# A macaron transformer layer: the first block product of each FFN gets its raw weights and weight sums in a small pool of its own, and its split operands in other buffers

## The chip, the cores and the metric

The kernel runs on one core of a Trainium2 chip. The metric is the device time of one execution in microseconds (us), as the median of several runs. The engines are named as in the profile: PE (matmuls), DVE (VectorE), ACT (ScalarE), POOL (GpSimd) and SP (which here only issues DMAs).

## The reference

One layer: a SwiGLU FFN, a mixer (stick-breaking attention and RWKV-7 side by side), and a second SwiGLU FFN, each between RMSNorms and added to the residual. The change touches the two FFNs alone:

```python
def swiglu(x, w_gate, w_up, w_down):
    return (jax.nn.silu(x @ w_gate) * (x @ w_up)) @ w_down

f = swiglu(rmsnorm(x, ffn1_pre_g[l]), ffn1_w_gate[l], ffn1_w_up[l], ffn1_w_down[l])
x = x + 0.5 * rmsnorm(f, ffn1_post_g[l])
m = hybrid_mixer(...)
x = x + rmsnorm(m, mix_post_g[l])
f = swiglu(rmsnorm(x, ffn2_pre_g[l]), ffn2_w_gate[l], ffn2_w_up[l], ffn2_w_down[l])
x = x + 0.5 * rmsnorm(f, ffn2_post_g[l])
```

Here x is 1024 tokens by 1024 channels in float32, and the hidden width is 2816.

## The kernel before

**Precision.** Every float32 matmul is made of three: each operand is split into a high part (`wh`, `xh`) and the rest (`wl`, `xl`), and `mm3` (lines 118 to 121) adds high x high, high x low and low x high. So each weight tile takes a rounding copy and a subtraction, nearly all of them on POOL (the copy on ACT for three of seven operands).

**The up phase.** The hidden width is 22 blocks of 128 (`f` = 0 to 21). Blocks 0 and 1 are *plain*: `plain_mm(f, h)` multiplies the whole gate and up weights of a block with half h of the tokens, and `plain_evac` takes SiLU(gate) x up to DRAM. Two of these four calls come before `up()`, two in it. Blocks 2 to 21 are *block products*: for each block, the gate and up weights and the two token halves form a 2 x 2 block matrix product, done with 7 half-size products (Winograd's form) in place of 8. One half-size product is 12 matmuls of 512 columns, a block takes 84. This needs sums on both sides:

- the **input sums**, once for each FFN: `combine()` (lines 231 to 267) makes them from the normalised input on DVE, with whole tiles of 128 x 2048 in a pool of five (`xr`), their high parts on ACT. It is a generator: `up()` runs it in three pieces between the plain products;
- the **weight sums**, once for each block: `prep(f)` (lines 291 to 309) makes S1 to S4 on DVE (128 x 512 each) from the raw weights that `load(f)` fetched (two DMAs of 512 KB on SP's queue), and then splits the seven operands in the order `PO` = 1, 2, 5, 6, 4, 7, 3: the high part on ACT for 2, 6 and 7, else on POOL (line 307), and the low part always on POOL (line 308).

`product(f)` (lines 368 to 393) runs the seven products and the evacuations between them; `evac1` takes the first two (`p1`), `u2`, `y5`, `u3` are later ones.

**Buffers.** Split operands go in pairs into a ring of six tile pairs (`slot`, lines 280 to 286). Pool `WP` is always open and has two raw tiles (`wr`) and four `wh`/`wl` pairs; the plain blocks fill exactly these four. Pool `fu` of the up phase holds the rest: two pairs, the raw weights of even blocks (`raw`; odd blocks use `wr`), the weight sums (`S`) and the evacuation tiles (`tp`). `fu` is opened only when `combine()` is through, since its addresses overlap those of `xr`. The line that decides which pairs of the ring lie where is

```python
if j == 0:
    pool = self.fu if i % 6 < 2 else WP
```

**The down phase** follows at once: `ffn_down` loads the down weights through `wr` (two tiles) and splits them on POOL into `WP`'s four pairs, every third one into a pool of its own (`EX`).

**What sets the order.** A scheduler orders each engine's instructions when the program is built, following the order of the code, data and buffer dependencies; buffers of a pool are handed on in order of release. Each engine, and SP's queue, then executes in that fixed order and waits at its head.

Of the kernel before, what the change touches and what calls it, by code (L numbers as in the profile page):

```python
# [13 lines left out]
ALU = mybir.AluOpType  # L14
# [4 lines left out]
P = 128  # L19
# [11 lines left out]
def layer_kernel(ctx: ExitStack, tc: tile.TileContext, a: dict, out: bass.AP, dbg=None):  # L31
# [182 lines left out]
    class Ffn:  # L214
# [54 lines left out]

        def load(self, f):  # L270
            c = slice(f * P, (f + 1) * P)
            pool, tag = (WP, "wr") if f % 2 else (self.fu, "raw")
            pair = []
            for i, w in enumerate((self.wg, self.wu)):
                t = pool.tile(tag, f"{self.nm}r{i}_{f}", [P, 1024]).rearrange("p (k c) -> p k c", c=P)
                nc.sync.dma_start(t, w[:, :, c])
                pair.append(t)
            self.raw[f] = pair

        def slot(self):  # L280
            i, j = divmod(self.nslot, 2)
            self.nslot += 1
            if j == 0:
                pool = self.fu if i % 6 < 2 else WP
                self.pair = [pool.tile(t, f"{self.nm}{t}_{i}", [P, 1024], F32R) for t in ("wh", "wl")]
            return [self.half(t, j) for t in self.pair]

# [2 lines left out]

        def prep(self, f):
            G, U = self.raw.pop(f)
            S = [self.fu.tile("S", f"{self.nm}S{f}_{i}", [P, 1024]) for i in range(2)]
            S1, S2, S3, S4 = [self.half(S[i // 2], i % 2) for i in range(4)]
            A11, A12, A21, A22 = G[:, 0:4], G[:, 4:8], U[:, 0:4], U[:, 4:8]
            tt = nc.vector.tensor_tensor
            tt(S1, A21, A22, op=ALU.add)
            tt(S2, S1, A11, op=ALU.subtract)
            tt(S3, A11, A21, op=ALU.subtract)
            tt(S4, A12, S2, op=ALU.subtract)  # L300
            src = {1: A11, 2: A12, 5: S1, 6: S2, 4: A22, 7: S3, 3: S4}
            for n in PO:
                wh, wl = self.slot()
                if n in (2, 6, 7):
                    nc.scalar.copy(wh, src[n])  # L305
                else:
                    nc.gpsimd.tensor_scalar(wh, src[n], 1.0, 0.0, op0=ALU.mult, op1=ALU.add)  # L307
                nc.gpsimd.tensor_tensor(wl, src[n], wh, op=ALU.subtract)  # L308
                self.op[f, n] = wh, wl
# [84 lines left out]

        def up(self):

            comb = self.combine()
            self.plain_mm(0, 1)
            self.plain_evac(0, 0)
            self.plain_evac(1, 0)  # L400
            next(comb)
            self.plain_mm(1, 1)
            next(comb)
            self.plain_evac(0, 1)
            self.plain_evac(1, 1)
            next(comb, None)
            self.fu = Pool(self.nm + "u", dict(raw=2, S=2, wh=2, wl=2, tp=8))
            self.load(2)
            self.load(3)
            self.prep(2)  # L410
            for f in range(2, NF):
                if f + 1 < NF:
                    self.prep(f + 1)
                if f + 2 < NF:
                    self.load(f + 2)
                self.product(f)
            self.store(NF - 1)
            self.fu.close()

    def ffn_down(pl, hp, F, gb, post, half=None):  # L420
        nm = F.nm
# [170 lines left out]
    WP = Pool("wp", dict(wr=2, wh=4, wl=4))  # L592
# [11 lines left out]
    for h in range(2):  # L604
        for p2 in range(2):
# [3 lines left out]
            for i in range(2):  # L609
                tt = h * 4 + p2 * 2 + i  # L610
# [11 lines left out]
            r = rsqrt_col(nm, ss, 1.0 / D, EPS, n=2)  # L622
            for i in range(2):
                tt = h * 4 + p2 * 2 + i
# [419 lines left out]
    S2 = [pb.const(f"S{i}", [P, 4, P]) for i in range(2)]  # L1044
# [383 lines left out]
```

## Time and profile before

| | us |
|---|---|
| median of 3 runs (2266.04 to 2268.66) | 2267.11 |
| the profiled execution | 2267.87 |
| span of its instructions | 2266.1 |
| PE busy in it | 2142.8 (95%) |
| POOL busy | 963.7 (43%) |
| DVE busy | 1102.3 (49%) |

The profile is of one execution; its own time lies 0.76 us above the median of the runs and 1.8 us above its span. PE is busy for 95% of the span, so the time is PE's work plus its idle stretches, and each idle stretch is read where it lies: on the timeline, the bracket at a row's end gives how long the engine stood still before that instruction and what released it. Busy shares of the other engines say little; what counts is when a given operand of theirs is ready.

### The profile page before, as it was taken

Reading aid. Unit: us, or ns where it says so; the run is one execution under the profiler, and the core shown is the slowest. Engines: PE = TensorE matmul, PEld = TensorE weight load, DVE = VectorE, ACT = ScalarE, POOL = GpSimd, SP = SyncE. Lnnn points to the kernel's source line nnn. Section 1 sums busy time; section 2 is a strip of 40 time slices with the busy share of each in tenths; the row PEclk is TensorE's granted clock in tenths of the full one; section 3 lists DMA queues with packets and bytes.
Section 4 is the critical chain, followed back from the end, with each engine's and each line's share of the span. In section 5 each row is a group of like instructions: output and inputs, shape, how many; then the busy total and the mean of one; then the engine's idle time right before and its main releaser. Section 6 shows DMA issues by size and latency. Waiting matters only on the chain.

```text
span 2266.1 us, 29554 instructions
## 1 busy us (share of the span) xinstructions
PE 2142.8 (95%) x11168; PEld 1764.5 (78%) x11168; DVE 1102.3 (49%) x1652; ACT 786.0 (35%) x1349; POOL 963.7 (43%) x875
## 2 busy tenths in 40 slices
PE   7799999999999999999999999899799999999998
PEld 5678888878887777777888887777678888878886
DVE  4743333322445555735617778636743333322446
ACT  3322222223224544324126667436322222222212
POOL 2476666644232364344311111231666666634323
PEclk8899999999999999999989999999899999999999
DMA  3233232245444353353763663343232222245444
GB/s 116 70 93 91 75 90 75 67 142 183 142 149 130 93 164 119 109 168 99 229 161 117 187 200 108 130 139 121 76 91 84 84 84 84 66 137 169 130 135 162
DMA packets 295277, 276.16 MB, mean 122 GB/s; under 512 B 29664, under 2 KB 237536, under 8 KB 295136
## 3 DMA queue, kind: packets, MB, share of 16 engines
q1 hardware_dynamic: 244304, 248.85, 35.8%
q10 hardware_dynamic: 50832, 25.43, 4.2%
q8 instruction: 88, 1.44, 0.3%
q14 instruction: 53, 0.43, 0.1%
HBM read 195.60 MB, written 78.64 MB: 121 GB/s over the span
## 4 chain that ended last, share of the span: by engine, by line
PE 78%; DVE 10%; POOL 4%; ACT 4%; issue 3%; DMA 1%; SPq 0%; DVEq 0%; ACTq 0%; POOLq 0%
PE f1d L120 3%; PE f1d L121 3%; PE f1d L119 3%; PE pj L119 3%; PE f2d L119 3%; PE f2d L120 3%; PE f2d L121 3%; PE pj L121 3%; PE pj L120 3%; PE f2X L119 2%; PE f2X L120 2%; PE f2X L121 2%; PE f1X L119 2%; PE f1X L121 2%; PE f1X L120 2%
## 5 line engine op out<-in xcount | busy, mean ns | idle before, releaser
L107 POOL TENSOR_SCALAR wh<-wr 128x1024 fp32r<-128x1024 f32 x87 | 112.1, 1289 | 480.3 <-PE f1d L121 152.8
L108 POOL TENSOR_TENSOR wl<-wr,wh 128x1024 fp32r<-128x1024 f32 x87 | 213.5, 2455 | 6.0 <-PE pj L121 0.2
L120 PE MATMUL f1d<-wl,f1hh 128*128 128x512 f32 x352 | 138.8, 394 | 3.9 <-POOL wl L108 3.9
L119 PE MATMUL f2d<-wh,f2hh 128*128 128x512 f32 x352 | 137.9, 392 | 4.7 <-issue 3.5
L121 PE MATMUL f1d<-wh,f1hl 128*128 128x512 f32 x352 | 138.6, 394 | 0.4 <-DVE f1hl L435 0.4
L119 PE MATMUL f1d<-wh,f1hh 128*128 128x512 f32 x352 | 138.1, 393 | 0.0
L120 PE MATMUL f2d<-wl,f2hh 128*128 128x512 f32 x352 | 137.7, 391 | 0.0
L121 PE MATMUL f2d<-wh,f2hl 128*128 128x512 f32 x352 | 137.4, 390 | 0.0
L308 POOL TENSOR_TENSOR f2wl<-f2S,f2wh 128x512 fp32r<-128x512 f32 x80 | 104.0, 1311 | 4.0 <-ACT f2wh L305 1.7
L308 POOL TENSOR_TENSOR f1wl<-f1S,f1wh 128x512 fp32r<-128x512 f32 x80 | 103.9, 1310 | 4.0 <-ACT f1wh L305 1.7
L433 ACT CAST f2hh<-f2r 128x768 fp32r<-128x768 f32 (+1 forms) x56 | 45.1, 808 | 165.8 <-PE f2d L120 109.1
L433 ACT CAST f1hh<-f1r 128x768 fp32r<-128x768 f32 (+1 forms) x56 | 45.1, 807 | 165.7 <-PE f1d L120 109.8
L435 DVE TENSOR_TENSOR f2hl<-f2r,f2hh 128x768 fp32r<-128x768 f32 (+1 forms) x56 | 55.8, 998 | 68.9 <-ACT f2hh L433 68.9
L435 DVE TENSOR_TENSOR f1hl<-f1r,f1hh 128x768 fp32r<-128x768 f32 (+1 forms) x56 | 56.5, 1008 | 66.5 <-ACT f1hh L433 66.5
L308 POOL TENSOR_TENSOR f2wl<-f2r,f2wh 128x512 fp32r<-128x512 f32 x60 | 86.0, 1440 | 2.3
L308 POOL TENSOR_TENSOR f1wl<-f1r,f1wh 128x512 fp32r<-128x512 f32 x60 | 85.9, 1439 | 2.3
L307 POOL TENSOR_SCALAR f1wh<-f1r 128x512 fp32r<-128x512 f32 x40 | 33.4, 837 | 114.8 <-DMA f1r<-in_ffn_w_gate_dram 60.3
L119 PEld LDWEIGHTS f2d<-wh,f2hh 128*128 128x128 f32 x352 | 66.4, 189 | 19.6 <-issue 3.9
L120 PEld LDWEIGHTS f1d<-wl,f1hh 128*128 128x128 f32 x352 | 66.9, 190 | 18.5 <-POOL wl L108 4.7
L121 PEld LDWEIGHTS f1d<-wh,f1hl 128*128 128x128 f32 x352 | 66.9, 190 | 14.7 <-DVE f1hl L435 0.8
L119 PEld LDWEIGHTS f1d<-wh,f1hh 128*128 128x128 f32 x352 | 66.8, 190 | 14.0
L307 POOL TENSOR_SCALAR f2wh<-f2r 128x512 fp32r<-128x512 f32 x40 | 33.4, 835 | 104.0 <-DMA f2r<-in_ffn_w_gate_dram 49.5
(1382 smaller groups left out, 6233.1 us busy)
## 6 DMA issues: line engine op xcount, KB each, us to landing
wr<-in_ffn_w_down_dram SPq DMA_DIRECT2D x44, 512.0 KB, 3.9
f1r<-f1h_d SPq DMA_DIRECT2D x48, 384.0 KB, 3.5
f2r<-f2h_d SPq DMA_DIRECT2D x48, 384.0 KB, 3.5
wr<-in_w_in_dram SPq DMA_DIRECT2D x27, 512.0 KB, 4.0
f1r<-in_ffn_w_gate_dram SPq DMA_DIRECT2D x20, 512.0 KB, 3.9
f1r<-in_ffn_w_up_dram SPq DMA_DIRECT2D x20, 512.0 KB, 4.0
f2r<-in_ffn_w_gate_dram SPq DMA_DIRECT2D x20, 512.0 KB, 3.9
f2r<-in_ffn_w_up_dram SPq DMA_DIRECT2D x20, 512.0 KB, 3.9
```

The source lines that it names most:

```text
L107: nc.gpsimd.tensor_scalar(wh, raw, 1.0, 0.0, op0=ALU.mult, op1=ALU.add)
L108: nc.gpsimd.tensor_tensor(wl, raw, wh, op=ALU.subtract)
L119: nc.tensor.matmul(ps, lhsT=lh, rhs=rh, start=first, stop=False, **kw)
L120: nc.tensor.matmul(ps, lhsT=lh, rhs=rl, start=False, stop=False, **kw)
L121: nc.tensor.matmul(ps, lhsT=ll, rhs=rh, start=False, stop=last, **kw)
L307: nc.gpsimd.tensor_scalar(wh, src[n], 1.0, 0.0, op0=ALU.mult, op1=ALU.add)
L308: nc.gpsimd.tensor_tensor(wl, src[n], wh, op=ALU.subtract)
L433: nc.scalar.copy(hh, raw)
L435: nc.vector.tensor_tensor(hl, raw, hh, op=ALU.subtract)
```

## The change

A new pool `fr` holds the raw weights of the even blocks and one tile of weight sums. It is opened, and the first load issued, at the start of `up()`, ahead of `combine()`'s pools. `prep(2)` moves from behind the input sums to behind their second piece, ahead of the evacuations of the last two plain products. S3 and S4 get no tile any more: they are written in place over the raw blocks A21 and A12, S4 only when operand 2 (which reads A12) has been split. The ring of six pairs starts in `WP`: the first four pairs of a phase are now the plain blocks' tiles, and the two in `fu` come last.

```diff
         def load(self, f):
-            pool, tag = (WP, "wr") if f % 2 else (self.fu, "raw")
+            pool, tag = (WP, "wr") if f % 2 else (self.fr, "raw")
...
-                pool = self.fu if i % 6 < 2 else WP
+                pool = self.fu if i % 6 >= 4 else WP
...
         def prep(self, f):
             G, U = self.raw.pop(f)
-            S = [self.fu.tile("S", f"{self.nm}S{f}_{i}", [P, 1024]) for i in range(2)]
-            S1, S2, S3, S4 = [self.half(S[i // 2], i % 2) for i in range(4)]
+            S = self.fr.tile("S", f"{self.nm}S{f}", [P, 1024])
+            S1, S2 = [self.half(S, i) for i in range(2)]
             A11, A12, A21, A22 = G[:, 0:4], G[:, 4:8], U[:, 0:4], U[:, 4:8]
+            S3, S4 = A21, A12
             tt = nc.vector.tensor_tensor
             tt(S1, A21, A22, op=ALU.add)
             tt(S2, S1, A11, op=ALU.subtract)
             tt(S3, A11, A21, op=ALU.subtract)
-            tt(S4, A12, S2, op=ALU.subtract)
             src = {1: A11, 2: A12, 5: S1, 6: S2, 4: A22, 7: S3, 3: S4}
             for n in PO:
+                if n == 3:
+                    tt(S4, A12, S2, op=ALU.subtract)
                 wh, wl = self.slot()
...
         def up(self):
+            self.fr = Pool(self.nm + "r", dict(raw=2, S=1))
+            self.load(2)
             comb = self.combine()
...
             next(comb)
+            self.prep(2)
             self.plain_evac(0, 1)
             self.plain_evac(1, 1)
             next(comb, None)
-            self.fu = Pool(self.nm + "u", dict(raw=2, S=2, wh=2, wl=2, tp=8))
-            self.load(2)
+            self.fu = Pool(self.nm + "u", dict(wh=2, wl=2, tp=8))
             self.load(3)
-            self.prep(2)
```

How this moves instructions shows in two places. The first is DVE at the end of the first FFN's input sums. `f1R`, `f1L` and `X_1l` are tiles of the input sums (128 x 2048), `f1e` the evacuations of the plain products (they read PSUM), `f1S` weight sums of block 2 (and, in the last rows, of block 3), `f1r_2` and `f1r_3` the raw weights of these blocks, `f1p` the first evacuation of product 2. Before:

```order
L251 TENSOR_TENSOR f1R_573<-f1R_575,f1R_573 128x2048
L253 TENSOR_TENSOR f1R_576<-X_1h,X_1l 128x2048
L344 TENSOR_TENSOR f1e_1_642<-f1pZ_1_528,f1e_1_642 128x512
L254 TENSOR_TENSOR f1R_577<-f1R_576,f1R_573 128x2048
...
L247 TENSOR_TENSOR f1L_572<-f1R_574,f1H_571 128x2048
L344 TENSOR_TENSOR f1e_1_646<-f1pZ_1_611,f1e_1_646 128x512
L247 TENSOR_TENSOR X_1l<-f1R_575,X_1h 128x2048
L297 TENSOR_TENSOR f1S_0_664<-f1r_2_658 128x512
...
L300 TENSOR_TENSOR f1S_1_693<-f1r_3_660,f1S_0_692 128x512
L358 TENSOR_TENSOR f1p_748<-f1Z_735,f1p_748 128x512
```

And now:

```order
L251 TENSOR_TENSOR f1R_580<-f1R_582,f1R_580 128x2048
L253 TENSOR_TENSOR f1R_583<-X_1h,X_1l 128x2048
L298 TENSOR_TENSOR f1S_649<-f1r_2_508 128x512
L254 TENSOR_TENSOR f1R_584<-f1R_583,f1R_580 128x2048
...
L247 TENSOR_TENSOR f1L_579<-f1R_581,f1H_578 128x2048
L299 TENSOR_TENSOR f1S_649<-f1S_649,f1r_2_506 128x512
L300 TENSOR_TENSOR f1r_2_508<-f1r_2_506,f1r_2_508 128x512
L304 TENSOR_TENSOR f1r_2_506<-f1r_2_506,f1S_649 128x512
L346 TENSOR_TENSOR f1e_1_676<-f1pZ_1_535,f1e_1_676 128x512
L346 TENSOR_TENSOR f1e_1_680<-f1pZ_1_618,f1e_1_680 128x512
L247 TENSOR_TENSOR X_1l<-f1R_582,X_1h 128x2048
L360 TENSOR_TENSOR f1p_749<-f1Z_736,f1p_749 128x512
```

The four weight sums of block 2 move ahead of the last input sum, the two evacuations that stood within the input sums move behind them, and `f1p` of product 2 no longer stands behind the sums of block 3.

The second place is SP's queue of loads at the same point (`f1r_2`, `f1r_3`, `f1r_4`: raw weights of blocks 2, 3 and 4, gate and up):

```order
-L276 DMA f1r_3_660<-in_ffn_w_gate_dram 128x8x128
-L276 DMA f1r_2_656<-in_ffn_w_gate_dram 128x8x128
-L276 DMA f1r_2_658<-in_ffn_w_up_dram 128x8x128
-L276 DMA f1r_3_662<-in_ffn_w_up_dram 128x8x128
-L276 DMA f1r_4_718<-in_ffn_w_gate_dram 128x8x128
-L276 DMA f1r_4_720<-in_ffn_w_up_dram 128x8x128
+L276 DMA f1r_2_506<-in_ffn_w_gate_dram 128x8x128
+L276 DMA f1r_2_508<-in_ffn_w_up_dram 128x8x128
+L276 DMA f1r_4_719<-in_ffn_w_gate_dram 128x8x128
+L276 DMA f1r_4_721<-in_ffn_w_up_dram 128x8x128
+L276 DMA f1r_3_690<-in_ffn_w_gate_dram 128x8x128
+L276 DMA f1r_3_692<-in_ffn_w_up_dram 128x8x128
```

Block 2's loads now come first, and block 4's stand ahead of block 3's; block 4's go into the buffers that block 2's leave. The second FFN has the same orders at the same points.

## Rows read from the trace of the kernel before

**Rows 1.** Waits of PE, whole span: reader, releaser, us in total, times, longest.

```profile
PE f1X L119 <- POOL f1wh L307: 6.7, 1, 6.7
...
PE f1d L120 <- POOL wl L108: 3.9, 2, 2.0
...
PE f1X L119 <- ACT f1u L378: 2.8, 1, 2.8
```

**Rows 2.** Timeline of PE, first FFN: start, us, instruction, [idle before, releaser].

```profile
93.16 0.79 PE L119 MATMUL f1X<-X_0h,f1wh 128*128 128x512 f32 x1 [6.65 <-POOL f1wh L307]
...
98.41 0.80 PE L121 MATMUL f1X<-X_0h,f1wl 128*128 128x512 f32 x1 [4.04 <-POOL f1wl L308]
...
102.55 0.39 PE L119 MATMUL f1Z<-X_0h,f1wh 128*128 128x512 f32 x1
...
126.00 0.39 PE L119 MATMUL f1Z<-X_0h,f1wh 128*128 128x512 f32 x1
...
147.10 0.39 PE L119 MATMUL f1Z<-X_0h,f1wh 128*128 128x512 f32 x1
...
166.14 0.39 PE L119 MATMUL f1Z<-X_0h,f1wh 128*128 128x512 f32 x1
```

**Rows 3.** One stretch: length, busy PE, PEld, DVE, ACT, POOL, granted clock, DMA.

```profile
98.40:102.60 4.20, 4.19 (x11) 3.36 (x12) 0.51 (x1) 0.06 (x1) 4.20 (x5) 0.55 0.07 20
```

**Rows 4.** Timeline of PE, second FFN, same places as in Rows 2.

```profile
1624.70 0.40 PE L119 MATMUL f2Z<-x2X2h,f2wh 128*128 128x512 f32 x1
...
1669.13 0.39 PE L119 MATMUL f2Z<-x2X2h,f2wh 128*128 128x512 f32 x1
```

**Rows 5.** Timeline of DVE, end of the first FFN's input sums.

```profile
76.53 0.68 DVE L344 TENSOR_TENSOR f1e<-f1pZ,f1e 128x512 f32<-128x512 f32 x1
...
85.94 2.28 DVE L260 TENSOR_TENSOR f1R<-f1R,f1R 128x2048 f32<-128x2048 f32 x1
...
90.34 2.28 DVE L247 TENSOR_TENSOR f1L<-f1R,f1H 128x2048 fp32r<-128x2048 f32 x1
92.55 0.68 DVE L344 TENSOR_TENSOR f1e<-f1pZ,f1e 128x512 f32<-128x512 f32 x1
...
96.55 0.68 DVE L298 TENSOR_TENSOR f1S<-f1S,f1r 128x512 f32<-128x512 f32 x1
97.27 1.65 DVE L300 TENSOR_TENSOR f1S<-f1r,f1S 128x512 f32<-128x512 f32 x1
```

**Rows 6.** Timeline of POOL, first operands of block 2.

```profile
85.67 7.43 POOL L307 TENSOR_SCALAR f1wh<-f1r 128x512 fp32r<-128x512 f32 x1 [60.34 <-DMA f1r<-in_ffn_w_gate_dram]
93.19 6.86 POOL L308 TENSOR_TENSOR f1wl<-f1r,f1wh 128x512 fp32r<-128x512 f32 x2
...
101.18 0.62 POOL L307 TENSOR_SCALAR f1wh<-f1S 128x512 fp32r<-128x512 f32 x1
101.77 1.29 POOL L308 TENSOR_TENSOR f1wl<-f1r,f1wh 128x512 fp32r<-128x512 f32 x1
```

**Rows 7.** Timeline of SP's queue: gate weights of blocks 3 and 2.

```profile
79.66 1.01 SPq L276 DMA_DIRECT2D f1r<-in_ffn_w_gate_dram  x2
```

**Rows 8.** Timeline of POOL, first down weights of the first FFN.

```profile
459.92 1.06 POOL L107 TENSOR_SCALAR wh<-wr 128x1024 fp32r<-128x1024 f32 x1 [2.18 <-PE f1X L120]
...
467.32 1.05 POOL L107 TENSOR_SCALAR wh<-wr 128x1024 fp32r<-128x1024 f32 x1 [3.85 <-DMA wr<-in_ffn_w_down_dram]
...
489.19 1.18 POOL L107 TENSOR_SCALAR wh<-wr 128x1024 fp32r<-128x1024 f32 x1 [2.94 <-DMA wr<-in_ffn_w_down_dram]
490.33 5.84 POOL L108 TENSOR_TENSOR wl<-wr,wh 128x1024 fp32r<-128x1024 f32 x2
```

**Rows 9.** Timeline of PE, last block product of the first FFN and down phase.

```profile
470.77 0.39 PE L119 MATMUL f1Z<-X_0h,f1wh 128*128 128x512 f32 x1
...
493.17 0.50 PE L120 MATMUL f1d<-wl,f1hh 128*128 128x512 f32 x1 [1.99 <-POOL wl L108]
```

**Rows 10.** Timeline of PE, first down matmul of the second FFN.

```profile
2012.83 0.47 PE L119 MATMUL f2d<-wh,f2hh 128*128 128x512 f32 x1 [3.54 <-issue]
```

More of the change, by code (lines that the diff above doesn't have):

```diff
@@ L418, in up @@
             self.fu.close()
+            self.fr.close()
     def ffn_down(pl, hp, F, gb, post, half=None):
```

## The prediction

> **What bounds the kernel now.** First the waits of PE over the whole span: since PE is busy for 95% of it, only these can be won. Those of the up phases lead: PE waits 6.7 us for the first `wh` of the first FFN's block 2, and later 2.8 us for the evacuation `f1u` [rows 1]. Then PE's timeline, where one start per product tells what the waits cost in all. I take the first matmul of operand 2 (`f1Z`). From block 4 on, products are 166.14 - 147.10 = 19.04 us apart: 84 matmuls at 0.227 us, nothing lost [rows 2]. Product 2 starts 6.65 us late (PE was ready at 93.16 - 6.65 = 86.51), stops 4.04 us more at its third matmul, and reaches operand 2 at 102.55 in place of 86.51 + 12 x 0.227 = 89.23: 13.3 us lost. Product 2 then takes 23.45 us (4.4 too many) and product 3 21.10 (2.1 too many) [rows 2]. That makes 19.8 us. The second FFN repeats it: 1624.70 to 1669.13 is 44.4 us, 102.55 to 147.10 is 44.6 [rows 2, 4]. So at most 39.6 us, 1.7%, are there to be won.
>
> Why is the first `wh` late? On POOL it takes 7.43 us, the same form elsewhere 0.62 [rows 6]. In that time DVE runs three input sums back to back, from 85.94 to 90.34 + 2.28 = 92.62 [rows 5]; POOL ends at 93.10, 0.48 after the last, while DVE runs an evacuation that reads PSUM. The next two, `wl`, take 6.86 in place of 2 x 1.29 [rows 6]; DVE is in sums again until 97.23, and the sum at 97.27, which needs the one just before it and so starts after a gap, in turn takes 1.65 in place of 0.68 [rows 5]. So in this trace POOL stands still while DVE's two-operand sums follow each other without a gap, across their boundaries, and gets in at a gap or under an evacuation.
>
> **The change part by part.**
>
> *Block 2's raw weights come early, and its operands go to free tiles.* The load is issued before the input sums begin and costs nothing there: SP's queue has only block 3's and 4's loads behind it. The first pair of the ring is the tile of plain block 0, free when its last matmul is through, some 13 us before 86.51 (48 plain matmuls of 0.227 us follow, 10.9 us, and a few more). So by its data POOL can split operand 1 at about 73.5 in place of 85.67.
>
> *But DVE does not let it.* The order shows what DVE has to do from there: input sums without a break, block 2's S1 among them at the place where an evacuation stood at 76.53 [rows 5]. That evacuation read PSUM and would have let POOL in; it now stands behind the sums, as does the one at 92.55. At 92.55 S2 follows, then S3, 0.60 us apart, until about 93.83; only S4 must wait, for POOL's split of operand 2. So I take POOL to get in at 93.83, and `wh` to be ready 0.48 later, at 94.3. **PE's first wait grows from 6.65 to 7.9 us.** What is won is the second: with DVE waiting for POOL, `wl` takes its 1.29 alone, until 95.6, and PE's third matmul stops 0.5 us in place of 4.04. The 10 matmuls to operand 2 took 102.55 - 98.41 = 4.14 us at a granted clock of 0.55 [rows 2, 3], the lower level, after PE had stood; the same again gives 99.8. Gain 2.75 us (were the clock up at once, 10 x 0.227, it would be 4.6).
>
> *Operands of block 2 behind these.* Eight more POOL operations remain, three of 0.62 and five of 1.29: 8.3 us from 96.9, plus at most 3 us for S4 and the last input sum (0.68 and 2.28) taking turns with them. They end at 105 to 108, each ahead of PE, which needs 2.72 us for an operand and does the last at 110. No wait here.
>
> *Product 2.* `f1u` was late because `f1p` stood on DVE behind block 3's sums, and these behind POOL; ACT's queue held SiLU of `f1p` ahead of the copy of `f1u`. Now `f1p` stands ahead of block 3's sums, and so the 2.8 us and the slow matmuls after them go. I keep 0.3 us, since the order puts only four matmuls between operands 6 and 7: gain 4.1 us. Product 3 then begins at 99.8 + 19.34 - 2.72 = 116.4; before, at 126.00 - 2.72 = 123.28.
>
> *Block 3's load moves behind block 4's on SP.* SP now stands at its head until POOL has made block 2's last operand (105 to 108), for block 4's buffers. Block 3's loads go out right behind. In the trace POOL got its data 5 to 6 us after the gate loads were issued at 79.66 and 80.2 [rows 6, 7], so 110.5 to 114.5; with a split of 1.9 us, operand 1 of block 3 is ready at 112.4 to 116.4, against 116.4 when PE comes. Just in time, with POOL then 3 us or less ahead. Of product 3's 2.1 us I count 1.5 as won, and let 0 and 2.1 stand as bounds.
>
> *Sum of an up phase:* 2.75 + 4.1 + 1.5 = 8.3 us, for both 16.7.
>
> *Where the phase ends, the ring's turn costs something.* The last pairs of the ring (66 to 69) now lie in `WP`, and all hold operands of block 21; before, two of `WP`'s four held operands of block 20. In the first FFN the down weights followed this chain: first split at 459.92, ready 467.32 - 3.85 = 463.47 (3.55 us), each further raw tile 3.85 us after a split has freed its buffer, and the operation that PE waits for at 493.17 begins at 490.33 and ends the second of 5.84 us [rows 8, 9]. Now the first split waits for operand 1 of block 21, done at 470.77 [rows 9]: ready 474.35; second raw 478.2, split 481.75; third raw 485.6, split 489.15; fourth raw 493.1, its `wh` 1.14, then the `wl` of 2.92: 497.2. That is 4.0 us later than 493.2, and PE has nothing else there. **Loss 4.0 us**, in the first FFN. In the second, POOL's order differs: product 21 ends at 2012.83 - 3.54 = 2009.29 [rows 10], so operand 1 is done at 1992.97, and the same steps give splits at 1996.5 and 2003.9, raw at 2007.75, and the `wl` that PE wants first at 2011.3. PE begins at 2012.83 for other reasons [rows 10], so this hides; without that cover it would cost up to 2 us.
>
> *At no cost:* the in-place sums are as many and as long as before. In the steady products S4 now waits for POOL's split of operand 2 of its own block; behind it on DVE stand the evacuations. POOL's ring runs up to 12 operands ahead of PE, 32 us, and I expect that wait to be over when DVE comes.
>
> Sum: 16.7 - 4.0 = 12.7 us less. Against the profiled execution, 2267.87 - 12.7 = 2255.2; that lies 0.76 above the median, so against the median **2254.4 us**.
>
> **A rule that speaks for more.** The trace shows POOL shut out over three DVE instructions in a row [rows 5, 6]. The Trainium skill (SBUF — State Buffer, Who interferes with whom) says that of two such instructions the second to issue fully blocks until the first finishes: by that, POOL's turn would come at the end of one DVE instruction, which the 7.43 us do not bear out. What that would give is the first rival.
>
> **The rivals.**
>
> *POOL gets turns between DVE's sums.* Then splitting starts near 74.4, POOL and DVE alternate, and operand 1 is there before 86.51. The input sums end some 7 us later, 5 to 6 POOL operations of 0.62 to 1.29 among them; operand 4, fourth in PE's new order, needs them at about 99.7 where PE comes at 94.7: 5 us lost, with 1.5 of slow matmuls. Product 2 ends near 112, and block 3's data, behind block 4's, come for 113.5: 1.5 more. Product 3 starts at about 114, with 1 us lost in it. Against 19.8 that is 9 lost, 10.9 won per phase: 2 x 10.9 - 4 = 17.8, so 2249.3. Against it stand four long POOL operations, two in each FFN, one of each kind shown.
>
> *Block 3 comes late.* If the loads take their turn one after the other behind block 4's, and POOL ends at 108, product 3 stops for 3.5 us more and its own waits stay: 8.3 - 3.5 = 4.8 per phase, 9.6 - 4 = 5.6 in all: 2261.5. For it: the queue's order, and a margin of 0 to 4 us only.
>
> *The change doesn't do what it says.* The first operand is not earlier, and product 2 and 3 keep their waits in a new form: 2 x 2.75 - 4 = 1.5 us, 2265.6, no difference. For it: the first wait grows.
>
> *Slower: the in-place sums stall the steady products.* S4 waits on DVE for POOL, an evacuation that frees a PSUM bank comes late, and PE stops in every block. From block 4 on there are 18 products per FFN, 36 in all; 12.7 / 36 = 0.35 us each eats the gain, and half a `wl`, 0.65 us, gives 36 x 0.65 - 12.7 = 10.7 slower: 2277.8. Against it: those products run without any loss now (19.04), and the ring's lead.
>
> **How the numbers follow.** My forecast 0.52 (2250 to 2259), turns between sums 0.15, late block 3 0.14, no earlier 0.11, stalls 0.08. A measurement of this kernel tells 0.2% (4.5 us) from no change: faster is below 2262.6. Faster: 0.52 + 0.15 and 0.10 of the late block, 0.77; same 0.04 + 0.11 = 0.15; slower 0.08. The range from 2247 to 2264 holds the first three and leaves out the last two, 0.19.
>
> **What would show it.** Right: PE's first wait for `f1wh` near 7.9 us and that for `f1wl` under 1; a POOL `wh` of some 20 us while DVE sums; no wait for `f1u`; product 3 beginning 7 us earlier; at the first down matmuls a wait for `wl` of 6 us in place of 1.99; from block 4 on 19.04 a product. Wrong: a first wait gone altogether (turns), a wait for block 3's `wh` or its load (late block), or products from block 4 on above 19.04 (stalls).

## The result, and the profile after it

The changed kernel takes **2287.11 us** (median of 6 runs, 2282.99 to 2290.88); the kernel before, beside it, 2267.84 us (6 runs, 2266.04 to 2270.37). The ratio is 1.0084, with a 95% interval from 1.0071 to 1.0097: slower by 0.8%, where 2254.4 us had been forecast. The profiled execution of the changed kernel is the fastest of its six: 2282.99 us, span 2281.3 us, against 2267.87 us and 2266.1 us before. So 15.1 us are to be found between the two traces. Of all executions below one was in a slow state (of e14_e6_evac_ahead, 3531.48 us at a granted clock of 0.55); its median counts it, its ratio does not.

The waits of PE in the whole span of the changed kernel (reader, releaser, us in total, times, longest) answer to [rows 1]:

```profile
PE f1X L119 <- ACT f1u L380: 10.9, 1, 10.9
PE f2X L119 <- ACT f2u L380: 10.9, 1, 10.9
PE f2X L119 <- POOL f2wh L309: 8.0, 1, 8.0
PE f1X L119 <- POOL f1wh L309: 7.7, 1, 7.7
...
PE f1d L120 <- POOL wl L108: 4.5, 2, 2.6
```

The first wait, for `wh`, is a little longer than before, in both FFNs. The one for `f1wl`, 4.04 us before [rows 2], has left the head of the list. New are two waits of 10.9 us for the evacuation `f1u`/`f2u`. Where they are, PE's timeline of the first FFN tells (start, us, instruction, idle before and releaser; compare [rows 2]):

```profile
95.53 0.79 PE L119 MATMUL f1X<-X_0h,f1wh 128*128 128x512 f32 x1 [7.71 <-POOL f1wh L309]
...
101.22 0.39 PE L119 MATMUL f1Z<-X_0h,f1wh 128*128 128x512 f32 x1
...
121.13 0.39 PE L119 MATMUL f1Z<-X_0h,f1wh 128*128 128x512 f32 x1
...
144.40 0.79 PE L119 MATMUL f1X<-X_1h,f1wh 128*128 128x512 f32 x1 [10.87 <-ACT f1u L380]
...
154.78 0.39 PE L119 MATMUL f1Z<-X_0h,f1wh 128*128 128x512 f32 x1
...
173.82 0.39 PE L119 MATMUL f1Z<-X_0h,f1wh 128*128 128x512 f32 x1
```

The first matmuls of operand 2 (`f1Z`) mark the products. PE has done the plain blocks at 95.53 - 7.71 = 87.82 (86.51 before). From there to product 2's mark it now takes 13.40 us, before 16.04; product 2 takes 19.91 us, before 23.45; **product 3 takes 33.65 us, before 21.10**; from then on 19.04, as before. The up phase, from PE's end of the plain blocks to product 4's mark, is 66.96 us in place of 60.59. The second FFN repeats it: 66.44 in place of 60.78. That is 12.0 of the 15.1 us. The rest lies outside: 1.3 us at the start of the kernel, 1.4 between the two up phases, 0.4 at the end.

Product 3's 33.65 us are 19.04 of work, two waits of 0.96 and 10.87, and 2.8 us more. Of these, 2.2 come behind the long wait, since PE's clock fell while it stood: the 36 matmuls from 144.40 to 154.78 take 10.38 us, at 0.227 us each they would take 8.17. One stretch (length, busy PE, PEld, DVE, ACT, POOL, granted clock, DMA) shows a mean of 0.78, between the two levels of 1.2 and 2.4 GHz. It is 0.56, near the lower one, until 149.5, and 1.00 from there on:

```profile
144.40:154.70 10.30, 10.30 (x36) 8.33 (x37) 4.18 (x6) 2.31 (x4) 7.77 (x8) 0.78 0.30 86
```

Why is `f1u` late? It is read backwards, from ACT through DVE to POOL and SP (timelines of these engines, first FFN):

```profile
142.75 0.63 ACT L361 ACTIVATE f1p<-f1p 128x512 f32<-128x512 f32 x1 [9.33 <-DVE f1p L360]
143.76 0.59 ACT L380 COPY f1u<-f1X 128x512 f32<-128x512 f32 x1
...
118.42 0.79 DVE L298 TENSOR_TENSOR f1S<-f1r 128x512 f32<-128x512 f32 x1 [13.50 <-DMA f1r<-in_ffn_w_up_dram]
...
135.12 1.09 DVE L304 TENSOR_TENSOR f1r<-f1r,f1S 128x512 f32<-128x512 f32 x1 [2.40 <-POOL f1wl L310]
140.38 1.74 DVE L298 TENSOR_TENSOR f1S<-f1r 128x512 f32<-128x512 f32 x1 [4.17 <-POOL f1wl L310]
142.04 0.68 DVE L360 TENSOR_TENSOR f1p<-f1Z,f1p 128x512 f32<-128x512 f32 x1
...
74.77 20.71 POOL L309 TENSOR_SCALAR f1wh<-f1r 128x512 fp32r<-128x512 f32 x1 [48.62 <-PE f1pX L120]
...
116.68 0.62 POOL L309 TENSOR_SCALAR f1wh<-f1r 128x512 fp32r<-128x512 f32 x1 [7.92 <-DMA f1r<-in_ffn_w_gate_dram]
...
109.26 0.55 SPq L276 DMA_DIRECT2D f1r<-in_ffn_w_gate_dram  x1
109.92 2.13 SPq L276 DMA_DIRECT2D f1r<-in_ffn_w_up_dram  x1
```

ACT copies `f1u` at 143.76 because SiLU of `f1p` stands ahead of it, and that waited 9.33 us for DVE. On DVE, `f1p` of product 3 (142.04) stands behind the last sum of block 4 (135.12) and the first of block 5 (140.38), and both wait for POOL. POOL is late with block 4 because it stood idle for 7.92 us until block 3's weights came, at 116.68, and DVE had nothing of block 3 until 118.42. Block 3's two loads were issued at 109.26 and 109.92, where the kernel before issued the first at 79.66 [rows 7]. And POOL's first operand took 20.71 us under DVE's sums. So the trace offers three causes in one chain: the order of the loads, the sums that wait for POOL, and POOL's late start. The experiments take them apart.

### The profile page after: what moved, and what is told of

It is laid out like the page before. It is cut to its first block, busy times and chain, and to the rows that moved or that the text cites. A ratio compares the mean times of both kernels' runs of the same rounds, so it can differ in the third digit from the quotient of the medians.

```text
span 2281.3 us, 29566 instructions
## 1 busy us (share of the span) xinstructions
PE 2144.1 (94%) x11168; PEld 1763.7 (77%) x11168; DVE 1100.1 (48%) x1652; ACT 786.1 (34%) x1349; POOL 1010.5 (44%) x875
## 4 chain that ended last, share of the span: by engine, by line
PE 76%; DVE 9%; issue 5%; POOL 4%; ACT 4%; DMA 2%; SPq 0%; DVEq 0%; ACTq 0%; POOLq 0%
PE f1d L120 3%; PE f1d L121 3%; PE f1d L119 3%; PE pj L119 3%; PE pj L121 3%; PE f2d L119 3%; PE f2d L120 3%; PE f2d L121 3%; PE pj L120 3%; PE f2X L119 2%; PE f2X L120 2%; PE f2X L121 2%; PE f1X L119 2%; PE f1X L120 2%; PE f1X L121 2%
## 5 line engine op out<-in xcount | busy, mean ns | idle before, releaser
L310 POOL TENSOR_TENSOR f2wl<-f2r,f2wh 128x512 fp32r<-128x512 f32 x100 | 138.5, 1401 | 3.2
L310 POOL TENSOR_TENSOR f1wl<-f1r,f1wh 128x512 fp32r<-128x512 f32 x100 | 136.5, 1382 | 3.2
L309 POOL TENSOR_SCALAR f1wh<-f1r 128x512 fp32r<-128x512 f32 x60 | 69.5, 1165 | 133.6 <-PE f1pX L120 48.6
L309 POOL TENSOR_SCALAR f2wh<-f2r 128x512 fp32r<-128x512 f32 x60 | 67.9, 1137 | 121.2 <-PE f2pX L120 36.8
L304 DVE TENSOR_TENSOR f2r<-f2r,f2S 128x512 f32<-128x512 f32 x20 | 15.8, 788 | 153.8 <-POOL f2wl L310 153.8
L304 DVE TENSOR_TENSOR f1r<-f1r,f1S 128x512 f32<-128x512 f32 x20 | 15.8, 788 | 153.7 <-POOL f1wl L310 153.7
L439 DVE TENSOR_TENSOR f2hl<-f2r,f2hh 128x768 fp32r<-128x768 f32 (+1 forms) x56 | 56.5, 1010 | 67.8 <-ACT f2hh L437 67.8
L119 PEld LDWEIGHTS f2d<-wh,f2hh 128*128 128x128 f32 x352 | 66.7, 189 | 19.5 <-issue 4.6
L120 PEld LDWEIGHTS f1d<-wl,f1hh 128*128 128x128 f32 x352 | 66.5, 189 | 18.8 <-POOL wl L108 5.3
L121 PEld LDWEIGHTS f1d<-wh,f1hl 128*128 128x128 f32 x352 | 66.5, 189 | 17.0 <-DVE f1hl L439 3.4
L121 PEld LDWEIGHTS f2d<-wh,f2hl 128*128 128x128 f32 x352 | 66.5, 189 | 14.3 <-DVE f2hl L439 0.5
```

What stands on the lines that cost most here:

```text
L119: nc.tensor.matmul(ps, lhsT=lh, rhs=rh, start=first, stop=False, **kw)
L120: nc.tensor.matmul(ps, lhsT=lh, rhs=rl, start=False, stop=False, **kw)
L121: nc.tensor.matmul(ps, lhsT=ll, rhs=rh, start=False, stop=last, **kw)
L439: nc.vector.tensor_tensor(hl, raw, hh, op=ALU.subtract)
```

## The experiments

Times are medians; each ratio is against the kernel before, measured beside it. "Up" is the up phase as defined above, first and second FFN, in the one profiled execution of each kernel.

| kernel | product 3 (1st FFN) | up, us | time, us | ratio, 95% interval |
|---|---|---|---|---|
| before | 21.10 | 60.6, 60.8 | 2267.5 to 2268.3 | |
| changed | 33.65 | 67.0, 66.4 | 2287.1 | 1.0084 [1.0071, 1.0097] |
| e1_load_order | 33.82 | 66.7, 66.5 | 2287.4 | 1.0090 [1.0075, 1.0105] |
| e4_own_s4 | 33.84 | 66.7, 66.5 | 2283.1 | 1.0075 [1.0057, 1.0092] |
| e3_evac_first | 26.63 | 58.2, 58.6 | 2268.0 | 1.0003 [0.9993, 1.0014] |
| e2_ring_only | 24.10 | 62.3, 64.2 | 2279.1 | 1.0053 [1.0037, 1.0070] |
| e6_block3_first | 27.44 | 60.0, 59.7 | 2273.2 | 1.0012 [0.9998, 1.0027] |
| e12_own_sums | 26.36 | 57.9, 58.1 | 2267.5 | 0.9987 [0.9973, 1.0002] |
| e11_first_two | 29.32 | 58.3, 58.9 | 2270.5 | 1.0007 [0.9995, 1.0020] |
| e13_both | 27.83 | 57.8, 57.6 | 2267.4 | 0.9999 [0.9985, 1.0012] |
| e14_e6_evac_ahead | 20.47 | 53.0, 53.3 | 2261.7 | 0.9972 [0.9958, 0.9986] |
| e15_e3_evac_ahead | 19.14 | 50.7, 50.9 | **2255.2** | 0.9936 [0.9911, 0.9961] |
| e16_e11_evac_ahead | 21.32 | 51.3, 51.7 | 2258.7 | 0.9959 [0.9945, 0.9974] |
| e17_before_evac_ahead | 19.04 | 56.5, 58.9 | 2264.9 | 0.9980 [0.9966, 0.9994] |

### First round: three suspects, and the ring

**e1_load_order.** Block 4's load is written behind product 2:

```
-                if f + 2 < NF:
+                if f > 2 and f + 2 < NF:
                     self.load(f + 2)
                 self.product(f)
+                if f == 2:
+                    self.load(f + 2)
```

> The changed kernel with one move: block 4's weight load is written behind the product of block 2, so that on SP the two loads of block 3 stand ahead of the two of block 4 again (as in the kernel before). In the changed kernel SP issues block 3's pair at 109.3 and 109.9 us, behind block 4's pair, which waits for POOL's last operand of block 2 (108.8 us); POOL then idles 7.9 us for block 3's weights and PE waits 10.9 us in product 3 of each up phase. Theory A (load order): POOL goes on with block 3 without a gap, everything behind it comes about 8 us sooner, the 10.9 us wait falls to 3 us or less in both phases, time about 2287 - 2 x 8 = 2271 us. Theory B (the fourth sum, now written in place, has DVE wait for POOL): DVE still stands behind POOL's low part of the second operand, the 10.9 us wait keeps at least 8 us, time above 2281 us. Theory C (POOL shut out by DVE's sums for 20.7 us at the start): the loads' order gives back only what POOL idled, and what is left of the 10.9 us, some 3 us, belongs to POOL's late start; the first wait of 7.7 us stays under all three.

Nothing moved: 2287.4 us, and PE's 10.9 us are there. But the edit did not do what it was meant to. The scheduler (the planner of the expectations), which sets the order of SP's queue, put block 4's loads ahead of block 3's again. So this run is a second measurement of the changed kernel and speaks for no theory. e6_block3_first makes the test.

**e4_own_s4.** From block 3 on the fourth sum has its own tile again:

```
             S3, S4 = A21, A12
+            if f > 2:
+                S4 = self.fu.tile("S4", f"{self.nm}T{f}", [P, 512]).rearrange("p (k c) -> p k c", c=P)
...
-                if n == 3:
+                if n == (3 if f == 2 else 1):
                     tt(S4, A12, S2, op=ALU.subtract)
...
-            self.fu = Pool(self.nm + "u", dict(wh=2, wl=2, tp=8))
+            self.fu = Pool(self.nm + "u", dict(wh=2, wl=2, tp=8, S4=1))
```

> The changed kernel, but from block 3 on the fourth weight sum has a tile of its own again (512 columns, in the pool opened behind the plain blocks) and is formed right behind the third, before any operand is cut, as in the kernel before; so DVE no longer waits there for POOL's low part of the second operand. Block 2 stays as changed. Theory A (load order: block 3's loads behind block 4's): the 10.9 us wait of PE in product 3 stays within 2 us, time 2283 to 2289 us. Theory B (the in-place sum holds DVE up, and the first evacuation of product 3, queued behind it, with it): the wait falls to 3 us or less in both phases, time about 2271 us. Theory C (POOL's late start) says as A.

The wait stayed at 10.9 us in both phases, and the up phases at 66.7 and 66.5. Theory B falls: the sum formed in place is not what holds product 3. Block 4's fourth sum no longer waits for POOL (2.40 us in the changed kernel), but block 5's first, behind it, now waits 5.99 us in place of 4.17. (That the time reads 4 us less has no place in the up phases.)

**e3_evac_first.** Block 2's sums are written behind the first of the last two plain evacuations:

```
             next(comb)
-            self.prep(2)
             self.plain_evac(0, 1)
+            self.prep(2)
             self.plain_evac(1, 1)
```

> The changed kernel with the sums of block 2 written behind the first of the last two plain evacuations instead of ahead of both; on DVE the two evacuations that read PSUM then stand inside the run of sums (one ahead of the first sum, one behind it), where the changed kernel has them behind all sums. Theory C (POOL shut out for 20.7 us by DVE's back-to-back sums of two SBUF operands): POOL gets in under the evacuations, its first high part ends well before 95 us (some 5 to 10 us sooner), PE's first wait of 7.7 us falls to 4 us or less, and as the loads of blocks 4 and 3 wait for POOL's end of block 2, product 3's wait of 10.9 us falls by as much as POOL gained; time 2287 - 2 x (4 to 8) = 2271 to 2279 us. Theory A (load order alone): the first wait may change, product 3's does not by more than 2 us. If the lock-out is not lifted by an evacuation, POOL's first high part takes 20 us as before and nothing moves.

2268.0 us: the whole loss is gone, more than theory C forecast. Timelines of POOL, DVE, PE and SP in this kernel:

```profile
74.00 3.64 POOL L309 TENSOR_SCALAR f1wh<-f1r 128x512 fp32r<-128x512 f32 x1 [48.37 <-PE f1pX L120]
77.73 18.86 POOL L310 TENSOR_TENSOR f1wl<-f1r,f1wh 128x512 fp32r<-128x512 f32 x2
...
77.08 0.69 DVE L346 TENSOR_TENSOR f1e<-f1pZ,f1e 128x512 f32<-128x512 f32 x1
...
93.70 0.68 DVE L346 TENSOR_TENSOR f1e<-f1pZ,f1e 128x512 f32<-128x512 f32 x1
...
94.95 0.80 PE L121 MATMUL f1X<-X_0h,f1wl 128*128 128x512 f32 x1 [7.44 <-POOL f1wl L310]
...
127.31 0.76 PE L119 MATMUL f1DY<-f1H,f1wh 128*128 128x512 f32 x1 [5.96 <-DVE f1v L386]
...
80.23 0.37 SPq L276 DMA_DIRECT2D f1r<-in_ffn_w_gate_dram  x1
96.84 0.37 SPq L276 DMA_DIRECT2D f1r<-in_ffn_w_up_dram  x1
```

The reader is to see three things. POOL's first `wh` ends at 77.64, in the 0.69 us in which DVE's evacuation (77.08) reads PSUM; where that evacuation was missing it took 20.71 us. The next operation is shut out in turn, until the second evacuation at 93.70, so PE's wait for `wh` goes and one of 7.44 us for `wl` comes, where theory C expected 4 us or less; the start gains only 1 us (12.5 us to product 2's mark, against 13.40). And block 3's loads go out at 80.23 and 96.84, each some 3 us behind the start of an evacuation. That is the link I had not seen: the plain evacuations write into the tiles `wr`, the same that then take block 3's raw weights, so the evacuation and its store to DRAM have to be through first. The change moved the evacuations behind block 2's sums, and block 3's loads with them. So this edit moves two things, POOL's turns and block 3's loads, which here stand ahead of block 4's again, and does not tell them apart; e6_block3_first does. In product 3, a wait of 5.96 us is left.

**e2_ring_only.** The kernel before with the ring's start alone:

```
-                pool = self.fu if i % 6 < 2 else WP
+                pool = self.fu if i % 6 >= 4 else WP
```

> The kernel before with one part of the change alone: where the ring of operand tiles starts (the first four pairs of a round in the plain blocks' tiles, the last two in the up pool's). The prediction priced this at 4.0 us lost in the down phase of the first FFN (the low part that the down product waits for comes from tiles freed later) and nothing in the second; that gives 2267.8 + 4 = 2272 us, with PE's wait for the down weights' low part at 5 us or more where the kernel before has 2.0. If the changed kernel's later start of the up phase is what moved the down phase, the ring alone costs nothing: 2266 to 2269 us. The up phase should keep its length within 1 us under both, since the sums still start behind the evacuations.

2279.1 us, more than either expectation, and in another place. Waits of PE, and POOL's timeline, in this kernel:

```profile
PE f1X L119 <- POOL f1wh L307: 12.3, 1, 12.3
...
94.84 3.94 POOL L308 TENSOR_TENSOR f1wl<-f1r,f1wh 128x512 fp32r<-128x512 f32 x1 [69.70 <-ACT f1wh L305]
98.75 1.05 POOL L307 TENSOR_SCALAR f1wh<-f1r 128x512 fp32r<-128x512 f32 x1
```

With other tiles the scheduler makes another order: POOL has the `wl` of the second operand ahead of the `wh` of the first, and PE's first wait is 12.3 us. So the up phases did not keep their length (+1.7 and +3.4 us), and this is no clean measure of the ring. On the term that I had priced it does speak: PE's wait for the down weights' low part is 1.76 us here, no longer than the 1.99 before [rows 9], though a wait of 1.90 us for `f1hl` stands ahead of it.

### Second round: block 3's loads, and what is left in product 3

**e6_block3_first.** The changed kernel, with each load pinned behind the one before it; in effect block 3's loads ahead of block 4's.

```
-                nc.sync.dma_start(t, w[:, :, c])
+                d = nc.sync.dma_start(t, w[:, :, c])
...
+            self.last = d
...
                 if f + 2 < NF:
-                    self.load(f + 2)
+                    with tc.issue_after(self.last.ins):
+                        self.load(f + 2)
```

> The changed kernel with each block's load pinned behind the load of the block before it on SP; in the order that leaves one difference, the two loads of block 3 ahead of the two of block 4, on every other engine the order is the changed kernel's but for POOL's names. (The edit called e1_load_order was meant to do this, but the planner kept block 4's loads in front.) Theory A2 (load order): what then releases block 3's loads are the stores of the last two plain evacuations, whose tiles are block 3's raw tiles: issued at 99.8 and 100.4 us, 2.5 us to landing, so block 3's loads go out at about 102.5 and 103 instead of 109.3 and 109.9; POOL's gap of 7.9 us shrinks to about 1, the 10.9 us wait in product 3 to about 4, and the time to 2287 - 2 x 6.8 = 2273 us. Theory C2 (POOL's late start alone, the gap filled by work that would be late anyway): the wait stays above 8 us, time above 2281 us.

2273.2 us, as theory A2 said. Timelines of SP, DVE and PE in this kernel:

```profile
101.97 0.37 SPq L276 DMA_DIRECT2D f1r<-in_ffn_w_gate_dram  x1
102.78 0.37 SPq L276 DMA_DIRECT2D f1r<-in_ffn_w_up_dram  x1
...
107.74 0.97 DVE L299 TENSOR_TENSOR f1S<-f1r 128x512 f32<-128x512 f32 x1 [2.69 <-DMA f1r<-in_ffn_w_up_dram]
...
131.91 1.75 DVE L299 TENSOR_TENSOR f1S<-f1r 128x512 f32<-128x512 f32 x1 [4.27 <-POOL f1wl L311]
133.69 0.98 DVE L300 TENSOR_TENSOR f1S<-f1S,f1r 128x512 f32<-128x512 f32 x1
134.60 0.68 DVE L361 TENSOR_TENSOR f1p<-f1Z,f1p 128x512 f32<-128x512 f32 x1
...
136.95 0.79 PE L119 MATMUL f1X<-X_1h,f1wh 128*128 128x512 f32 x1 [4.51 <-ACT f1u L381]
```

The loads go out 7.2 us sooner, DVE has block 3 at 107.74 in place of 118.42, and product 3 falls from 33.65 to 27.44 us. POOL's first operand still takes 20.23 us here, so the 6.2 us won in product 3 were the order of the loads and not POOL's late start. What is left, 4.51 us, is `f1p` on DVE (134.60) behind a sum of block 5 that waits 4.27 us for POOL.

**e12_own_sums** is e3_evac_first with more tiles for the sums, meant to keep them from waiting for POOL; **e11_first_two** is e3_evac_first with the first two operands of block 2 split by ACT and DVE; **e13_both** joins them.

```
-            S = self.fr.tile("S", f"{self.nm}S{f}", [P, 1024])
+            S = (self.fu if f % 2 else self.fr).tile("S", f"{self.nm}S{f}", [P, 1024])
...
+            if f > 2:
+                S4 = self.fu.tile("S4", f"{self.nm}T{f}", [P, 512]).rearrange("p (k c) -> p k c", c=P)
...
+            if f > 2:
+                tt(S4, A12, S2, op=ALU.subtract)
...
-                if n == 3:
+                if n == 3 and f == 2:
...
-            self.fu = Pool(self.nm + "u", dict(wh=2, wl=2, tp=8))
+            self.fu = Pool(self.nm + "u", dict(wh=2, wl=2, tp=8, S4=1, S=1))
```

```
+        def first(self, f):
+            G = self.raw[f][0]
+            for n, a in ((1, G[:, 0:4]), (2, G[:, 4:8])):
+                wh, wl = self.slot()
+                nc.scalar.copy(wh, a)
+                nc.vector.tensor_tensor(wl, a, wh, op=ALU.subtract)
+                self.op[f, n] = wh, wl
...
+                if (f, n) in self.op:
+                    continue
...
             self.plain_mm(1, 1)
+            self.first(2)
             next(comb)
```

> The kernel of e3_evac_first, and from block 3 on the fourth sum in a tile of its own and the sums S1, S2 of odd blocks in a second tile, so that the sums of blocks 3 and 4 wait for no operand on POOL. In e3_evac_first PE waits 6.0 us in product 3 for an evacuation that stands on DVE behind the sums of block 4, two of which wait 4.4 and 3.6 us for POOL. Theory B2 (in product 3 it is DVE's sums waiting for POOL that hold the evacuations up): that wait falls to 2 us or less in both phases, time 2268 - 2 x 4 = 2260 us. Theory A3 (the sums of block 4 wait for block 4's weights as long as for POOL): they wait for the load instead, the wait of PE stays above 4 us, time 2264 to 2269 us. PE's wait of 7.4 us for the first low part stays under both.

> The kernel of e3_evac_first, but block 2's first two operands are split by ACT (high part) and DVE (low part), written ahead of the second piece of the input sums, so that POOL, shut out by the sums until 94 us, is not needed for what PE wants first. Theory C (POOL's lock-out sets PE's first wait): PE's waits for the first high and low part (7.7 us in the changed kernel, 7.4 us for the low part in e3_evac_first) both go, the third operand comes at about 97 us; product 3's wait grows by what DVE's queue cannot follow, some 3 us; time 2268 - 2 x 4 = 2260 us. If the two low parts on DVE (2 x 0.7 us) lengthen the sums that PE waits for, a wait for an input sum appears and the time is 2266 us or more.

> Both of the above together (first two operands of block 2 off POOL, own tiles for the later sums). Under theories B2 and C the two gains add up: time 2268 - 2 x (7.4 + 3) = 2247 us, up phase (from PE's end of the plain products to the start of product 4's second operand) about 48 us against 58.2 in e3_evac_first, 60.6 in the kernel before and 67.0 in the changed one. If what holds product 3 up is block 4's load, the time is 2255 to 2262 us.

None of the three beats the kernel before by more than its interval. e12_own_sums lies in the range of theory A3; e11_first_two (2270.5 us) misses the 2260 of theory C, and e13_both (2267.4) both of its forecasts, 2247 and 2255 to 2262. DVE in e12_own_sums, then PE in e11_first_two:

```profile
115.17 1.33 DVE L300 TENSOR_TENSOR f1S<-f1r 128x512 f32<-128x512 f32 x1 [8.03 <-DMA f1r<-in_ffn_w_up_dram]
...
123.43 1.74 DVE L304 TENSOR_TENSOR f1T<-f1r,f1S 128x512 f32<-128x512 f32 x1 [4.22 <-POOL f1wl L314]
...
125.69 0.68 DVE L390 TENSOR_TENSOR f1v<-f1DW,f1v 128x512 f32<-128x512 f32 x1
```

```profile
96.14 0.50 PE L119 MATMUL f1DY<-f1H,f1wh 128*128 128x512 f32 x1 [2.63 <-POOL f1wh L319]
98.82 0.79 PE L121 MATMUL f1DY<-f1H,f1wl 128*128 128x512 f32 x1 [1.94 <-POOL f1wl L320]
...
126.74 0.77 PE L119 MATMUL f1DY<-f1H,f1wh 128*128 128x512 f32 x1 [7.00 <-DVE f1v L396]
```

In e12_own_sums block 4's first sum waits 8.03 us for block 4's load, as A3 said. But the edit did not take the sums off POOL: there is one tile for the fourth sum (`f1T`), and block 4's waits 4.22 us until POOL has split block 3's out of it. Product 2's evacuation `f1v`, which PE needs in product 3, stands behind it on DVE, at 125.69. PE's wait is 5.5 us, against 6.0. So B2 was not tested: a wait for POOL still stands right ahead of the evacuation (6.05 us in e13_both). Whether the load or POOL holds the sums, `f1v` stands behind them; that order is what the third round changes.

In e11_first_two both first waits go, as theory C said, but PE now waits 2.63 and 1.94 us for the third operand, in product 2, and 7.00 for `f1v` in product 3. What is won at the start is given back there: up 58.3 against 58.2. So PE's first wait is POOL's lock-out, but taking it away alone is worth nothing. That is not only DVE's queue: with that queue put right too (e16_e11_evac_ahead below) up is 51.3, against 50.7 in e15_e3_evac_ahead without the early split.

### Third round: the queue on DVE

One edit, on four kernels: the sums of blocks 4 to 6 are queued on DVE behind the evacuation `f1v` of the product two blocks earlier (`self.behind`), which the scheduler had put behind the sums.

```
-            nc.vector.tensor_tensor(u3, w, u3, op=ALU.add)
+            self.behind = nc.vector.tensor_tensor(u3, w, u3, op=ALU.add)
...
-                if f + 1 < NF:
+                if 3 <= f < 6:
+                    with tc.issue_after(self.behind.ins):
+                        self.prep(f + 1)
+                elif f + 1 < NF:
                     self.prep(f + 1)
```

> The kernel of e3_evac_first with one difference: the sums of blocks 4 to 6 are queued on DVE behind the first two evacuations that end the product two blocks earlier, where the planner had put them ahead. In e3_evac_first and e12_own_sums PE waits 6.0 and 5.5 us in product 3 for such an evacuation of product 2, whether or not the sums wait for POOL; what is left are block 4's weights. Theory E (DVE's queue: the sums of block 4 stand ahead of product 2's evacuations and wait for block 4's load): that wait goes, product 3 takes 20 to 21 us instead of 26.6, in both phases, time 2268 - 2 x 6 = 2256 us. Theory F (POOL is late in any case, its operands for product 3 come no sooner): a wait for a high or low part takes the place of the 6.0 us, time 2264 to 2269 us.

> The same edit on the kernel of e6_block3_first (the changed kernel with block 3's loads ahead of block 4's). There PE still waits 4.5 us in product 3 for an evacuation behind the first one of product 3 on DVE, which stands behind block 4's last sum and block 5's first; both wait for POOL. Theory E: the 4.5 us fall to 1 or less, time 2273 - 2 x 4 = 2265 us, PE's first wait of 7.2 us stays. Theory F: a wait for an operand of POOL takes its place, time above 2270 us. Against the changed kernel (2287 us) the two moves of order together would then have brought back all that product 3 lost.

> The same edit on the kernel of e11_first_two (first two operands of block 2 off POOL), where PE waits 7.0 us in product 3 for product 2's evacuation. Theory E: that wait goes, product 3 takes 21 to 22 us instead of 29.3, time 2270.5 - 2 x 7 = 2256 us. Theory F: a wait for POOL's operands takes its place, time 2264 us or more.

> The same edit on the kernel before, without any part of the change. Its product 3 takes 21.1 us against 19.04 in the steady products, so theory E allows 2 us per phase: 2267.8 - 4 = 2264 us; if the planner's order costs nothing there (POOL is earlier, block 4's load comes at 103 us), the time stays within 0.1% of the kernel before.

All four came out as theory E said, within 4 us: 2255.2, 2261.7, 2258.7 and 2264.9 us. DVE and PE in e15_e3_evac_ahead:

```profile
115.27 0.68 DVE L386 TENSOR_TENSOR f1v<-f1DW,f1v 128x512 f32<-128x512 f32 x1
...
117.65 1.09 DVE L298 TENSOR_TENSOR f1S<-f1r 128x512 f32<-128x512 f32 x1
...
126.61 0.68 DVE L360 TENSOR_TENSOR f1p<-f1Z,f1p 128x512 f32<-128x512 f32 x1
...
118.15 0.39 PE L119 MATMUL f1Z<-X_0h,f1wh 128*128 128x512 f32 x1
...
137.29 0.39 PE L119 MATMUL f1Z<-X_0h,f1wh 128*128 128x512 f32 x1
```

`f1v` is through at 115.95, ahead of block 4's sum, and product 3 takes 137.29 - 118.15 = 19.14 us, with no wait. No wait for an operand took its place (theory F falls). e14_e6_evac_ahead is the changed kernel with nothing but two corrections of order, SP's loads and DVE's queue. PE's timeline in it:

```profile
120.09 0.39 PE L119 MATMUL f1Z<-X_0h,f1wh 128*128 128x512 f32 x1
...
140.56 0.39 PE L119 MATMUL f1Z<-X_0h,f1wh 128*128 128x512 f32 x1
```

Product 3 falls to 20.47 us, with a wait of 1.1 us for `f1p` left, and with it the change is faster than the kernel before, by 0.28%. e17_before_evac_ahead shows the same queue on the kernel before: 0.20%, with product 3 at 19.04 in both FFNs. So the corrected kernels are fairly compared with e17_before_evac_ahead. The interval of e14_e6_evac_ahead overlaps that one's, so it is not shown that the change itself wins anything there; the interval of e15_e3_evac_ahead lies below it. The fastest is e15_e3_evac_ahead, 0.64% faster than before; of its up phases only PE's waits for the first low part, 7.4 and 7.6 us, are left.

## Why the prediction was wrong

**The steps that held.** PE's first wait grew from 6.65 to 7.71 us (7.9 forecast; 8.00 in the second FFN), with POOL's `wh` at 20.71 us (some 20). The wait for `wl` went: to product 2's mark 16.04 - 13.40 = 2.64 us won (2.75 forecast). `f1u`'s wait in product 2 went: 23.45 - 19.91 = 3.54 us won, 4.02 in the second FFN (4.1 forecast). Products from block 4 on stayed at 19.04.

**The step that failed is product 3**, in "Block 3's load moves behind block 4's on SP". It was to win 1.5 us; it lost 33.65 - 21.10 = 12.55 and, in the second FFN, 33.63 - 20.94 = 12.69. Against the forecast that is 28 us, and the forecast missed by 32.7 us. The step followed the late load only to the first operand of block 3, and there it came out right, just in time: PE stood 0.47 us at 118.71. In part that was luck: POOL began on block 3 at 116.68, past the bound of 114.5 for its data, but PE too came 2.0 us after the forecast, at 118.4. The step did not follow the load on to DVE. There block 3's sums, block 4's last and block 5's first stand in a row, and `f1p` of product 3 behind them; each wait in that row (for the load, then twice for POOL) shifts `f1p`. In the order of instructions this could have been read beforehand, for product 3 as I had read it for product 2, where exactly such a queue was the 4.1 us I counted as won. Moving block 2 out of the way moved the same queue one product on, with a later load at its head.

Two bounds of that step were also wrong. Product 3 was given 0 to 2.1 us of gain, so no loss at all, and the rival that did name the place, "Block 3 comes late", was priced at 3.5 us per phase in place of 14. Its order on SP is shown to be half of the cause: e6_block3_first, which turns that order round, takes product 3 from 33.65 to 27.44 us. But PE stopped for an evacuation and not, as that rival has it, for block 3's operands. The other 7.0 us are DVE's queue: e14_e6_evac_ahead takes product 3 to 20.47. The text also did not see that block 3's weights go into the tiles of the plain evacuations, and so can't be loaded before these have been stored (101.97 in e6_block3_first, against 79.66 before [rows 7]). In the changed kernel itself this cost nothing more, since SP stood until 108.79 for block 4's tiles.

**The waits of the in-place sum.** "I expect that wait to be over when DVE comes" is refuted. The group of the fourth sums (count, busy and mean ns, then the idle time ahead of them and its releaser) in the changed kernel:

```profile
L304 DVE TENSOR_TENSOR f1r<-f1r,f1S 128x512 f32<-128x512 f32 x20 | 15.8, 788 | 153.7 <-POOL f1wl L310 153.7
```

DVE waits 153.7 / 20 = 7.7 us for POOL in a block, on average. It costs nothing from block 4 on, since the products keep their 19.04, so the slower rival, "the in-place sums stall the steady products", falls too. The kernel came out on that rival's side, but by another mechanism.

**The ring's price.** Forecast: 4.0 us in the first down phase, by a wait of 6 us for `wl`. Measured: that wait is 2.58 us. Ahead of it are two of 1.90 and 0.67 us, for `f1hl` on DVE, where before there was one of 0.43. In all PE stands 5.3 us there, against 2.4 before: 2.9 us of waiting. So the term was 1.1 us too large, and that it came near was luck: most of the added wait is for another operand, and e2_ring_only says the same (1.76 for `wl`, 1.90 for `f1hl`). Which step of DVE makes `f1hl` late was not tried.

**What stays open.** The up phases explain 12.0 us, the medians differ by 19.3. About 3 us are the waits at the first down matmuls. (Of these only 1.5 show in the length of the traced down phase: late in it, behind a wait of 1.90 us, the clock fell in the kernel before, 0.83 from 690 to 700, and not in the changed one, 1.00 from 701 to 711.) For the rest, the traces differ by several us outside the up phases. Between the first FFN's last product and the second's up phase the changed kernel takes 1122.5 us and e1_load_order, the same in these queues, 1126.1; 3.4 us of this difference lie in the last 120 us, where the granted clock was 0.99 and 0.97. Against the kernel before, the median of every kernel with the new ring is 4 to 9 us longer than its up phases account for, that of e17_before_evac_ahead, with the old ring, 3 us. What of this is the ring's was not settled.

## What to carry to other kernels

When a load or an operation moves, follow it through every in-order queue it feeds, for the next two or three rounds of the loop: the wait taken away here sat, larger, in the same queue one product later. Ask of each buffer who wrote it last; here a tile shared by an evacuation and the next load tied SP to DVE. And put an operation that PE waits for ahead of one whose data come later: that move of order alone was worth 0.2% on the kernel before, 0.4 to 0.7% on the others.

## What the runs showed of the hardware

DVE's sums with two inputs in SBUF, back to back, shut POOL out for longer than had been traced before: 20.71 and 20.23 us for an operation of 0.62 us, over some ten of DVE's instructions. One DVE instruction that reads PSUM, 0.69 us long, lets it in: in e3_evac_first POOL's operation ends at 77.64, 0.56 us after that instruction's start. The Trainium skill (SBUF — State Buffer, Who interferes with whom) says that a DVE instruction with at most one SBUF input, outside its 2-port modes, does not contend with GpSimd, and the trace agrees. So in these kernels the place of an evacuation among the sums decides when POOL starts.

A second point is the time that a load takes. Issued right behind another block's pair, block 3's second load reached DVE 118.42 - 109.92 = 8.5 us later; with only its own pair's first load just ahead of it, in e6_block3_first, 107.74 - 102.78 = 5.0 us later.
